# Sparse attention: two query tiles move from in front of the heads to beside them, and maxima, exponentials and value products change places in a step

## The chip, the cores and the metric

The kernel runs on one core of one Trainium2 chip. The metric is the time of one execution on the device in microseconds (us); lower is better. The kernel before took 1767.51 us in the median of three executions (1764.67 to 1768.47).

## What is computed

The reference is a decoder trunk of two layers over 256 positions of width 1024. Layer 0 is a latent attention with 16 heads and a feed-forward of product-key experts. From its output one set of keys and values is computed, for three branches. Layer 1 is the sparse attention with which the change has to do, and another expert feed-forward. Every sub-layer ends in a layer norm.

The sparse attention has 16 heads in 4 groups; the heads of a group share keys and values. Each head attends in three ways, and the results are added with sigmoid gates:

```
sc = q @ k_cmp;  p_c = masked_softmax(sc);  o_c = p_c @ v_cmp     # 15 compressed blocks
sc = q_rot @ k_g;  p_s = masked_softmax(sc);  o_s = p_s @ v_g     # selected blocks of 64 keys
sc = q_rot @ k_w;  p_w = masked_softmax(sc);  o_w = p_w @ v_w     # window of 512
out = gate0 * o_c + gate1 * o_s + gate2 * o_w
```

With 256 positions there are 4 blocks and up to 16 may be selected, so the selected branch sees every earlier key, as the window does. The kernel therefore handles both as plain causal attention with keys of their own (`br` 0 and 1). `q_rot` is the query after rotary embedding, `q` the one before. The compressed keys and values come out of a small two-layer network with a GELU over blocks of 32 tokens.

## The kernel before, in words

All large products are done as three TensorE products of a high and a low part: ScalarE rounds a float32 tile to its high part (`hi`, L119), VectorE subtracts it for the low part (`lo`, L130). Weights come through SP's DMA queue as a stream in a fixed order into four raw slots; `nxt()` takes the next tile, splits tiles ahead of it in `prep()`, and the low part of a tile frees a raw slot and so releases the next load. Each engine works strictly in the order in which the program was written; that order is written by hand.

The order around the change in `nsa` is kept by two counters. `tick()` counts one up for each weight tile or step, and `defer(n, f)` puts a piece of work n ticks later. Rotary embedding (`rope_T`) multiplies on VectorE, adds on GpSimd, and then goes through DRAM to change its layout: the store to `bounce` is issued one tick later, the load (`kr` for keys, `qr` for queries) two ticks later, both on SP. `k_split` (L1331) and `q_split` (L1342) then make high and low parts of the rotated keys and queries: casts on ScalarE, subtractions on VectorE.

There are eight query tiles, two for each group of four heads. `q_tile(i)` multiplies the residual stream with one; behind the second tile of a group come the copy `qu` and the rope. Tiles 0 to 3 stand between the four parts of `compress`, which fills the hidden layer of the compressed branch; then come tile 4, `mk_hid`, tile 5, `mk_kc` and `mk_hr` (the rest of the small network), and then a loop of 19 steps `st`. In step `st` TensorE computes the scores of head `st` (L1490 to L1498, `s0` and `s1`), transposes the scaled probabilities of head `st - 2` (two sets of three, L1500 to L1505), and in even steps from 4 on multiplies the probabilities of two heads with their values (`pvp`, L1507 on). VectorE takes the maxima of head `st` (L1523, L1524), ScalarE the exponentials (L1528, L1531), and VectorE or GpSimd scales head `st - 1` (L1541). `beside` names what else stands in a step: query tiles 6 and 7 in steps 0 and 2, and from step 6 on the output projection, one piece (`out_step`) in each even step. `cmp_at` names the four parts of the compressed branch (`cmp_scores`, `cmp_exp`, `cmp_sum`, `cmp_T`), once for each half of the heads, from steps 0 and 4 on. `out_close` ends the projection and makes the layer norm.

`self.ps()` takes one of four PSUM banks; a step's `s0`, its two sets of transposes, `pvp`, the query tiles and the compressed branch all take theirs there. `s1` has two banks of its own.

Of the kernel before, what the change touches and what calls it, by code (L numbers as in the profile page):

```python
# [12 lines left out]
F32 = mybir.dt.float32  # L13
# [5 lines left out]
AF = mybir.ActivationFunctionType  # L19
OP = mybir.AluOpType  # L20
AX = mybir.AxisListType
# [3 lines left out]
P = 128  # L25
# [18 lines left out]
class Kern:  # L44
# [1187 lines left out]
    def nsa(self, hN, gb):  # L1232
# [4 lines left out]
        with es:  # L1237
# [81 lines left out]
            for br in range(2):  # L1319
# [17 lines left out]
                self.defer(5, k_split)  # L1337
# [13 lines left out]
            def q_tile(i, tick=True):  # L1351
# [6 lines left out]
                def after():  # L1358
                    if hf == 1:
# [4 lines left out]
                        self.defer(4, lambda: q_split(g))  # L1364
# [93 lines left out]
            q_tile(4)()  # L1458
            mk_hid()
            q_tile(5)()  # L1460
            mk_kc()
            mk_hr()
# [4 lines left out]
            self.out_open(oT, hN, gb, False, 2, (x4, "x4"))  # L1467
            beside = {0: lambda: q_tile(6, False), 2: lambda: q_tile(7, False)}
            for k in range(KC - 2):
                beside[2 * k + 6] = lambda k=k: self.out_step(k)  # L1470
            cmp_at = {}
            for hb, s0_ in ((0, 0), (1, 4)):
                for i, f in enumerate((cmp_scores, cmp_exp, cmp_sum, cmp_T)):
                    cmp_at[s0_ + i] = lambda f=f, hb=hb: f(hb)
            pr, pts = {}, {}
            for st in range(NH + 3):
# [16 lines left out]
                cmp_at.get(st, lambda: None)()  # L1493
                if st == 1:
                    mk_vc()
                h = st - 2
                if 0 <= h < NH:
                    p, m = pr.pop(h)  # L1498
                    pT = prob.tile([P, 2, 384], F32, tag="pT", name="pT")
                    for br in range(2):  # L1500
                        ps = self.ps()
                        for i in range(3):
                            self.tr(ps[:, i * P:(i + 1) * P], p[:, br, i * P:(i + 1) * P])
                        nc.scalar.copy(pT[:, br, :], ps[:, 0:384])
                    pts[h] = pT  # L1505
                h = st - 3
                if 0 <= h < NH and h % 2 == 1:  # L1507
# [12 lines left out]
                h = st  # L1520
                if h < NH:
                    m = self.small.tile([P, 4, 4], F32, tag="m", name="m", bufs=4)
                    nc.vector.tensor_reduce(m[:, 0, 0:2], s0v, axis=AX.X, op=OP.max)  # L1523
                    nc.vector.tensor_reduce(m[:, 0, 2:4], s1v, axis=AX.X, op=OP.max)  # L1524
# [125 lines left out]
```

## Time and profile before

| | |
|---|---|
| median of three executions | 1767.51 us |
| profiled execution | 1764.78 us, span from the first to the last instruction 1763.0 us |
| mean granted clock of TensorE, share of full speed | 0.990 |
| TensorE busy | 1719.8 us (98%) |
| VectorE busy | 1554.6 us (88%) |
| ScalarE busy | 1043.3 us (59%) |
| GpSimd busy | 486.9 us (28%) |
| heads of the sparse attention, first scores to the last value products | 922.45 to 1005.05 us |

Times in the profile count from the first instruction. "PE" is TensorE, "PEld" its weight loads, "DVE" VectorE, "ACT" ScalarE, "POOL" GpSimd, "SPq" SP's DMA queue. L196 is the helper that issues every product, L225 the one for transposes, so tiles tell them apart: `ks,qs` are scores, `hT,hi` and `hT,lo` a query tile, `ident,p` transposes of probabilities, `pcT,vcp` and `pT,vN` value products. A busy TensorE may run at half clock, so its granted clock is read beside it. Matmuls overlap each other, so a row's start is compared with the next row's start.

### The profile page before, as it was taken

To read this page: it belongs to the slowest core of one execution; us is meant where nothing else is said; L and a number is where in the kernel's file an instruction comes from. 1 tells how busy PE (TensorE), PEld (TensorE's weight loads), DVE (VectorE), ACT (ScalarE), POOL (GpSimd) and SP (SyncE) were. 2 spreads that over 40 slices of the span, in tenths; PEclk is the share of its full clock that TensorE was granted. 3 is DMA by queue.
4 is the path that set the end of the run, shared out by engine and by line. 5 is a ranking of instruction groups with operands and counts; after the bars stand their busy time and mean duration, and the time that the engine had idled before them with its cause. 6 is when DMAs were issued, how large, how long until landed. Compare 5 with 4: busy or idle time off the path is not lost.

```text
span 1763.0 us, 30707 instructions
## 1 busy us (share of the span) xinstructions
PE 1719.8 (98%) x10610; PEld 1493.1 (85%) x10610; DVE 1554.6 (88%) x3675; ACT 1043.3 (59%) x2267; POOL 486.9 (28%) x441
## 2 busy tenths in 40 slices
PE   7999999999999999999898999999999999999997
PEld 6879999888888888888786789998888888888886
DVE  6778988988998999999677789988889997999998
ACT  6646555766666555556365755556666665655554
POOL 2110002000001777661341210001000005777840
PEclk9999999999999999999998999999999999999999
DMA  7535667555556899998571265657555557999992
GB/s 249 171 132 183 201 189 258 185 177 180 177 181 239 338 400 371 362 354 318 186 250 61 94 206 179 200 189 270 170 182 185 179 181 288 380 379 363 376 366 107
DMA packets 118619, 416.66 MB, mean 236 GB/s; under 512 B 16032, under 2 KB 18112, under 8 KB 117376
## 3 DMA queue, kind: packets, MB, share of 16 engines
q1 hardware_dynamic: 88976, 322.60, 53.6%
q0 software_dynamic: 29488, 92.10, 13.9%
q8 instruction: 84, 1.38, 0.3%
q14 instruction: 71, 0.58, 0.1%
HBM read 400.49 MB, written 13.63 MB: 235 GB/s over the span
## 4 chain that ended last, share of the span: by engine, by line
PE 88%; DVE 5%; DMA 3%; ACT 2%; issue 1%; POOL 0%; SPq 0%; ACTq 0%
PE mm L196 48%; PE acc L196 39%; PE mm L225 1%; DVE lo L130 1%; DMA raw<-p_wq 1%; ACT hi L119 1%; DMA actD<-gst 1%; DVE bnst L271 0%; DMA xT<-xT 0%; DMA raw<-s_wT 0%; POOL row L468 0%; DVE hN L293 0%; DVE hN L275 0%; DVE hN L268 0%; DMA spare<-p_v 0%
## 5 line engine op out<-in xcount | busy, mean ns | idle before, releaser
L196 PE MATMUL mm<-hT,hi 128*128 128x256 f32 (+1 forms) x3360 | 838.1, 330 | 0.0
L196 PE MATMUL mm<-hT,lo 128*128 128x256 f32 x2376 | 638.1, 280 | 1.3 <-DVE lo L130 1.3
L119 ACT CAST hi<-raw 128x1024 fp32r<-128x1024 f32 (+1 forms) x464 | 485.4, 1049 | 249.5 <-PE acc L196 102.6
L196 PEld LDWEIGHTS mm<-hT,hi 128*128 128x128 f32 x3360 | 553.4, 189 | 49.4 <-issue 1.2
L130 DVE TENSOR_TENSOR lo<-raw,hi 128x1024 fp32r<-128x1024 f32 (+1 forms) x460 | 562.1, 1225 | 35.5 <-ACT hi L119 30.8
L196 PEld LDWEIGHTS mm<-hT,lo 128*128 128x128 f32 x2376 | 448.3, 189 | 15.5 <-DVE lo L130 1.9
L196 PE MATMUL acc<-hi,W 128*128 128x512 f32 x1476 | 414.6, 389 | 0.3 <-ACT W L761 0.3
L196 PEld LDWEIGHTS acc<-hi,W 128*128 128x128 f32 x1476 | 276.9, 188 | 58.2 <-ACT W L761 0.7
L196 PE MATMUL acc<-lo,W 128*128 128x512 f32 x984 | 303.3, 389 | 0.3 <-issue 0.3
L750 POOL DMA_DIRECT2D actD<-gst x64 | 34.8, 544 | 793.5 <-ACT gst L748 793.4
L468 POOL DMA_INDIRECT row<-p_v,gidx x128 | 189.7, 1482 | 111.6 <-DVE gacc L482 63.8
L196 PEld LDWEIGHTS acc<-lo,W 128*128 128x128 f32 x984 | 184.5, 188 | 39.6 <-issue 0.9
L119 ACT CAST hi<-spare 128x1024 fp32r<-128x1024 f32 x125 | 131.3, 1051 | 115.2 <-PE acc L196 90.5
L472 POOL DMA_INDIRECT gel<-actD,gidx x128 | 172.7, 1349 | 50.2 <-issue 37.8
L482 DVE SCALAR_TENSOR_TENSOR gacc<-row,gw,gacc 128x1024 f32<-128x1024 f32 x126 | 161.5, 1282 | 1.1
L130 DVE TENSOR_TENSOR lo<-spare,hi 128x1024 fp32r<-128x1024 f32 x125 | 152.7, 1222 | 7.6 <-ACT hi L119 5.0
L742 ACT ACTIVATE mm<-mm 128x192 f32<-128x192 f32 (+23 forms) x170 | 40.9, 241 | 122.5 <-DVE mm L740 122.5
L766 DVE TENSOR_TENSOR W<-A,W 128x128 fp32r<-128x128 f32 (+1 forms) x512 | 108.1, 254 | 1.8 <-ACT W L761 1.8
L740 DVE TENSOR_TENSOR mm<-mm,half 128x256 f32<-128x256 f32 x174 | 74.7, 429 | 16.3 <-ACT half L739 15.8
L761 ACT CAST W<-A 128x192 fp32r<-128x192 f32 x256 | 88.2, 346 | 0.0
L643 DVE SCALAR_TENSOR_TENSOR A<-acc,A 128x176 f32<-128x176 f32 (+16 forms) x268 | 56.0, 274 | 34.2 <-PE acc L196 31.2
L745 ACT ACTIVATE A<-mm 128x192 f32<-128x192 f32 (+23 forms) x244 | 67.5, 277 | 7.7 <-DVE mm L740 2.6
(275 smaller groups left out, 1771.5 us busy)
## 6 DMA issues: line engine op xcount, KB each, us to landing
raw<-p_u SPq DMA_DIRECT2D x256, 512.0 KB
spare<-p_v SPq DMA_DIRECT2D x64, 1024.0 KB
raw<-p_v SPq DMA_DIRECT2D x63, 1024.0 KB
raw<-p_wq SPq DMA_DIRECT2D x32, 512.0 KB
actD<-gst POOLq DMA_DIRECT2D x64, 128.0 KB
raw<-b_wo SPq DMA_DIRECT2D x12, 512.0 KB
raw<-a_wo SPq DMA_DIRECT2D x8, 512.0 KB
raw<-s_wT SPq DMA_DIRECT2D x8, 512.0 KB
```

What stands on the lines that cost most here:

```text
L119: self.nc.scalar.copy(self.his[i], self.raws[i])
L130: e.tensor_tensor(self.los[i], raw, self.his[i].bitcast(F32), op=OP.subtract)
L196: self.nc.tensor.matmul(out, a, b, start=start, stop=stop)
L468: nc.gpsimd.indirect_dma_start(out=t, out_offset=None, in_=gtable, in_offset=bass.IndirectOffsetOnAxis(ap=gidx[:, 0, c:c + 1], axis=0))
L472: nc.gpsimd.indirect_dma_start(out=gel[c // 4][:, c % 4:c % 4 + 1], out_offset=None, in_=gplaces, in_offset=bass.IndirectOffsetOnAxis(ap=g ...
L482: nc.vector.scalar_tensor_tensor(gacc, t, gw[:, c:c + 1], gacc, op0=OP.mult, op1=OP.add)
L643: nc.vector.scalar_tensor_tensor(y, pv[:, j0:j0 + m], 1.0 / GS, y, op0=OP.mult, op1=OP.mult)
L740: nc.vector.tensor_tensor(ps[:, 0:S], ps[:, 0:S], t, op=OP.add)
L742: nc.scalar.activation(ps[:, 0:n], ps[:, 0:n], AF.Gelu)
L745: nc.scalar.activation(y[:, n:ND], ps[:, n:ND], AF.Gelu)
L761: nc.scalar.copy(WW[j][:, 0:ND], slot(j))
L766: nc.vector.tensor_tensor(WW[j][:, o:o + c.stop - c.start], slot(j)[:, c], WW[j][:, c].bitcast(F32), op=OP.subtract)
```

## The change

- `k_split` runs 4 ticks (branch 0) and 3 ticks (branch 1) behind its rope, where it was 5; `q_split` 2 ticks for group 0 and 3 for the others, where it was 4.
- Tiles 4 and 5, `mk_hid`, `mk_kc` and `mk_hr` leave the place in front of the loop. The four tiles 4 to 7 stand in steps 0, 1, 3 and 5; `mk_hid` in step 0, `mk_kc` and `mk_hr` in step 1, `mk_vc` in step 2. The compressed branch's parts begin in steps 2 and 6, where they began in 0 and 4.
- Maxima and exponentials are a function, `reduce_exp`. In steps 0 to 5 it stands in front of the compressed branch's parts; from step 6 on behind the transposes.
- The value products stand in front of the transposes of their step, where they stood behind them; the first pair comes in step 5 and not 4. The first piece of the output projection comes in step 7 and not 6.

```diff
--- before.py
+++ after.py
@@ -1334,7 +1334,7 @@
                     nc.scalar.copy(ks[64:128, :, br, :], ks[0:64, :, br, :].bitcast(F32))
                     nc.scalar.copy(klo[64:128, :, br, :], klo[0:64, :, br, :].bitcast(F32))
 
-                self.defer(5, k_split)
+                self.defer(4 - br, k_split)
 
 
             raws, qs = {}, {}
@@ -1361,7 +1361,7 @@
                         raws[g] = tmp.tile([64, HG, S], F32, tag="raw4", name="qr")
                         nc.scalar.copy(qu[:, g].rearrange("p a t -> p (a t)"), ps)
                         self.rope_T(tmp, ps.rearrange("p (a t) -> p a t", a=2), rT, raws[g])
-                        self.defer(4, lambda: q_split(g))
+                        self.defer(2 if g == 0 else 3, lambda: q_split(g))
                 return after
 
             def compress(hp, q):
@@ -1455,24 +1455,36 @@
                     self.tr(tp[:, tt * P:(tt + 1) * P], pc[:, tt, H8(hb), :].rearrange("p h c -> p (h c)"))
                 nc.scalar.copy(pcT[:, hb, :], tp[:, 0:S])
 
-            q_tile(4)()
-            mk_hid()
-            q_tile(5)()
-            mk_kc()
-            mk_hr()
             self.warm(AF.Exp)
 
 
             oT = [big.tile([P, KC, S], F32R, tag="big", name="oT") for _ in range(2)]
-            self.out_open(oT, hN, gb, False, 2, (x4, "x4"))
-            beside = {0: lambda: q_tile(6, False), 2: lambda: q_tile(7, False)}
+            self.out_open(oT, hN, gb, False, 4, (x4, "x4"))
+            beside = {st: lambda i=i: q_tile(4 + i, False) for i, st in enumerate((0, 1, 3, 5))}
             for k in range(KC - 2):
-                beside[2 * k + 6] = lambda k=k: self.out_step(k)
-            cmp_at = {}
-            for hb, s0_ in ((0, 0), (1, 4)):
+                beside[2 * k + 6 + (k == 0)] = lambda k=k: self.out_step(k)
+
+            cmp_at = {0: [mk_hid], 1: [mk_kc, mk_hr], 2: [mk_vc]}
+            for b8_, s0_ in ((0, 2), (1, 6)):
                 for i, f in enumerate((cmp_scores, cmp_exp, cmp_sum, cmp_T)):
-                    cmp_at[s0_ + i] = lambda f=f, hb=hb: f(hb)
+                    cmp_at.setdefault(s0_ + i, []).append(lambda f=f, b8_=b8_: f(b8_))
+            pv_at = {2 * k + 4 + (k == 0): 2 * k + 1 for k in range(NH // 2)}
             pr, pts = {}, {}
+
+            def reduce_exp(h, s0v, s1v):
+                m = self.small.tile([P, 4, 4], F32, tag="m", name="m", bufs=4)
+                nc.vector.tensor_reduce(m[:, 0, 0:2], s0v, axis=AX.X, op=OP.max)
+                nc.vector.tensor_reduce(m[:, 0, 2:4], s1v, axis=AX.X, op=OP.max)
+                nc.vector.tensor_scalar(m[:, 1, :], m[:, 0, :], -scale, None, op0=OP.mult)
+                p = prob.tile([P, 2, 384], F32, tag="p", name="p")
+                for br in range(2):
+                    nc.scalar.activation(p[:, br, 0:P], s0v[:, br, :], AF.Exp, bias=m[:, 1, br:br + 1], scale=scale,
+                                         accum_out=m[:, 2, br:br + 1])
+                for br in range(2):
+                    nc.scalar.activation(p[:, br, P:384], s1v[:, br, :], AF.Exp, bias=m[:, 1, 2 + br:3 + br], scale=scale,
+                                         accum_out=m[:, 2, 2 + br:3 + br])
+                pr[h] = (p, m)
+
             for st in range(NH + 3):
                 self.tick()
                 h = st
@@ -1490,21 +1502,12 @@
                     self.mm(s0v, self.identb, self.cmask, False, True)
                     self.mm(s1v[:, :, P:S], self.identb, self.cmask, False, True)
                 after = beside.get(st, lambda: None)() or (lambda: None)
-                cmp_at.get(st, lambda: None)()
-                if st == 1:
-                    mk_vc()
-                h = st - 2
-                if 0 <= h < NH:
-                    p, m = pr.pop(h)
-                    pT = prob.tile([P, 2, 384], F32, tag="pT", name="pT")
-                    for br in range(2):
-                        ps = self.ps()
-                        for i in range(3):
-                            self.tr(ps[:, i * P:(i + 1) * P], p[:, br, i * P:(i + 1) * P])
-                        nc.scalar.copy(pT[:, br, :], ps[:, 0:384])
-                    pts[h] = pT
-                h = st - 3
-                if 0 <= h < NH and h % 2 == 1:
+                if st < 6:
+                    reduce_exp(st, s0v, s1v)
+                for f in cmp_at.get(st, ()):
+                    f()
+                h = pv_at.get(st)
+                if h is not None:
                     pvp = self.ps()
                     pp = [pts.pop(h - 1), pts.pop(h)]
                     hb, g = h // 8, h // HG
@@ -1517,20 +1520,18 @@
                             self.mm(o[e], vN[:, 0, c:c + 64], pp[e][:, br, 0:S], False, False)
                         for e in range(2):
                             self.mm(o[e][:, P:S], vN[:, 1, c:c + 64], pp[e][:, br, S:384], False, br == 1)
-                h = st
-                if h < NH:
-                    m = self.small.tile([P, 4, 4], F32, tag="m", name="m", bufs=4)
-                    nc.vector.tensor_reduce(m[:, 0, 0:2], s0v, axis=AX.X, op=OP.max)
-                    nc.vector.tensor_reduce(m[:, 0, 2:4], s1v, axis=AX.X, op=OP.max)
-                    nc.vector.tensor_scalar(m[:, 1, :], m[:, 0, :], -scale, None, op0=OP.mult)
-                    p = prob.tile([P, 2, 384], F32, tag="p", name="p")
+                h = st - 2
+                if 0 <= h < NH:
+                    p, m = pr.pop(h)
+                    pT = prob.tile([P, 2, 384], F32, tag="pT", name="pT")
                     for br in range(2):
-                        nc.scalar.activation(p[:, br, 0:P], s0v[:, br, :], AF.Exp, bias=m[:, 1, br:br + 1], scale=scale,
-                                             accum_out=m[:, 2, br:br + 1])
-                    for br in range(2):
-                        nc.scalar.activation(p[:, br, P:384], s1v[:, br, :], AF.Exp, bias=m[:, 1, 2 + br:3 + br], scale=scale,
-                                             accum_out=m[:, 2, 2 + br:3 + br])
-                    pr[h] = (p, m)
+                        ps = self.ps()
+                        for i in range(3):
+                            self.tr(ps[:, i * P:(i + 1) * P], p[:, br, i * P:(i + 1) * P])
+                        nc.scalar.copy(pT[:, br, :], ps[:, 0:384])
+                    pts[h] = pT
+                if 6 <= st < NH:
+                    reduce_exp(st, s0v, s1v)
                 h = st - 1
                 if 0 <= h < NH:
                     p, m = pr[h]
@@ -1541,8 +1542,8 @@
                             eng.tensor_scalar(p[:, br, c], p[:, br, c], m[:, 3, 2 * tt + br:2 * tt + br + 1],
                                               gates[:, tt, 16 * br + 16 + h:16 * br + 17 + h], op0=OP.mult, op1=OP.mult)
                 after()
-                h = st - 3
-                if 0 <= h < NH and h % 2 == 1:
+                h = pv_at.get(st)
+                if h is not None:
                     self.split(oT[0][:, h // 2, :], oT[1][:, h // 2, :], pvp[:, 0:S])
             self.out_close()
 
```

## Rows read from the trace of the kernel before

**Rows 1.** The profile's chain that ended last, share of the span by engine.
```profile
PE 88%; DVE 5%; DMA 3%; ACT 2%; issue 1%; POOL 0%; SPq 0%; ACTq 0%
```

**Rows 2.** Windows: stretch, its length, busy us by engine (instructions), clock, DMA share, GB/s.
```profile
core 0: us, PE busy (x) PEld busy (x) DVE busy (x) ACT busy (x) POOL busy (x), PEclk, DMA share, GB/s
914.00:976.00 62.00, 52.59 (x333) 42.07 (x330) 47.94 (x113) 39.67 (x117) 9.48 (x12) 0.83 0.26 80
976.00:996.00 20.00, 19.17 (x139) 13.82 (x139) 14.89 (x40) 17.85 (x64) 10.42 (x12) 1.00 0.25 79
```

**Rows 3.** Timeline of TensorE, first heads: start, duration, instruction, [idle before <- releaser].
```profile
914.15 0.50 PE L196 MATMUL mm<-hT,hi 128*128 128x256 f32 x2
...
919.96 0.99 PE L196 MATMUL mm<-hidT,w2k 128*128 128x60 f32 x8
922.45 0.36 PE L196 MATMUL mm<-ks,qs 128*128 128x256 f32 x1 [1.49 <-DVE qs L1347]
...
927.86 1.90 PE L196 MATMUL mm<-kcp,qu 128*128 128x64 f32 x16
```

**Rows 4.** Timeline of SP's DMA queue: rope stores and loads of two groups.
```profile
908.06 0.38 SPq L1191 DMA_DIRECT2D bounce<-ropeO  x1
...
912.41 0.45 SPq L1192 DMA_DIRECT2D qr<-bounce  x1
...
925.86 0.39 SPq L1191 DMA_DIRECT2D bounce<-ropeO  x1
...
928.26 0.45 SPq L1192 DMA_DIRECT2D qr<-bounce  x1
```

**Rows 5.** Windows around the landing of group 0's query, columns as in rows 2.
```profile
913.50:915.00 1.50, 1.50 (x15) 1.03 (x12) 1.47 (x4) 0.22 (x1) 0.52 (x1) 1.00 0.57 175
915.00:918.00 3.00, 3.00 (x29) 3.00 (x28) 2.27 (x3) 2.92 (x5) 0.92 (x2) 1.00 0.00 0
```

**Rows 6.** Timeline of VectorE in the first heads, columns as in rows 3.
```profile
924.77 1.20 DVE L1404 COPY hidR<-hidT 128x240 f32<-128x240 f32 x2
...
935.38 1.29 DVE L1414 TENSOR_TENSOR vcp<-mm,m 128x512 f32<-128x512 f32 x2
936.59 0.41 DVE L1523 TENSOR_REDUCE m<-mm 128x2 f32<-128x256 f32 x1
...
937.71 0.17 DVE L1538 RECIPROCAL m<-m 128x4 f32<-128x4 f32 x1
...
939.08 1.23 DVE L130 TENSOR_TENSOR lo<-raw,hi 128x1024 fp32r<-128x1024 f32 x1
...
960.11 1.29 DVE L1347 TENSOR_TENSOR qs<-qr,qs 64x512 fp32r<-64x512 f32 x2 [0.92 <-ACT qs L1346]
```

**Rows 7.** Timeline of TensorE, one steady cycle of two heads, and the end.
```profile
974.09 0.38 PE L196 MATMUL mm<-ks,qs 128*128 128x256 f32 x1
...
975.12 0.82 PE L225 MATMUL mm<-ident,p 128*128 128x128 f32 x6
976.24 0.39 PE L196 MATMUL mm<-ks,qs 128*128 128x256 f32 x1 [0.30 <-ACT pT L1504]
...
978.68 0.82 PE L225 MATMUL mm<-ident,p 128*128 128x128 f32 x6
979.43 0.65 PE L196 MATMUL mm<-pcT,vcp 128*64 128x256 f32 x4
...
981.31 0.39 PE L196 MATMUL mm<-ks,qs 128*128 128x256 f32 x1
...
995.92 0.39 PE L196 MATMUL mm<-ks,qs 128*128 128x256 f32 x1
...
1005.05 0.73 PE L196 MATMUL acc<-hi,oT 128*128 128x512 f32 x2
```

**Rows 8.** Timeline of ScalarE in the same cycle.
```profile
972.78 0.38 ACT L1528 ACTIVATE p<-mm,m 128x128 f32<-128x128 f32 x1
...
974.37 0.40 ACT L214 CAST oT<-mm 128x256 fp32r<-128x256 f32 x1
975.70 0.86 ACT L1504 COPY pT<-mm 128x384 f32<-128x384 f32 x2 [0.93 <-PE mm L225]
```

## The prediction

> **What bounds the kernel now.** I read the chain of waits first: matmuls hold 88% of it [rows 1], so a change counts by what it does to TensorE's order, and a microsecond lost or won there is carried to the end. Then the windows of the sparse-attention stage. From 914 to 976 us TensorE is busy for 52.59 of 62 us at a mean granted clock of 0.83; the clock has two levels, 1.2 and 2.4 GHz, so a third of that stretch ran at the lower one. From 976 to 996 it is busy for 19.17 of 20 us at 1.00 [rows 2]. Two different stages stand side by side: a start of some 60 us, in which the first ten heads are slowed by short chains through VectorE and ScalarE, and a steady stretch that is full. The change acts on both, and the signs differ.
>
> **The front: heads before query tiles 4 and 5.** Before, TensorE takes up tile 4 at 914.15, is through with tiles 4 and 5, the transposes of `hb` and `mk_kc` at 920.95 (919.96 + 0.99), and waits 1.49 us for the split query of head 0 [rows 3]. After, head 0's scores come at 914.15 in its order, and 6.8 us (920.95 - 914.15) of ready work stand behind them. What is late next is the rotated query of group 0. It goes through DRAM: SP stores it at 908.06 and loads it at 912.41 [rows 4], and the data move until 915.0 [rows 5]. The `k_split` of branch 0, one tick sooner, puts three casts of ScalarE in front of the copy on which this rope waits; the key's load then ends about when they could start, and I put the delay of the copy at 0.4 us, an estimate. The second `k_split`, two ticks sooner, fills time in which ScalarE waits anyway and leaves GpSimd's rope more alone, which gives about as much back. I take a landing at 914.6. Bounds: with a store 0.8 us sooner and two trips of 2.40 us (store 925.86 to load 928.26, with little traffic [rows 4]) it lands at 912.1; with a store 0.7 us late and two trips of 4.35 at 917.5. I stay near the row of the same transfer. A cast and a subtraction of one half of the query (about 0.65 each, from the pair in [rows 6]) and 0.15 follow: scores at 916.05, between 914.15 and 918.9. TensorE waits 1.9 us where it waited 1.49. While ScalarE and VectorE stand in `q_split`, the rope of group 1 and the GELU wait behind it on both; the 6.8 us of TensorE's work cover them. Price: +0.4 us.
>
> [...]
>
> **The stretch from head 0 to head 10,** with starts in us. Head 0 916.05, 1.03 for its six products (975.12 - 974.09, [rows 7]). Tile 4 then takes 4.3 and not 2.8: before, the scores of head 0 and the tile behind them took 5.41 (927.86 - 922.45) instead of 1.03 + 2.8 (half of the 5.81 from 914.15 to 919.96, less a transpose), because the clock fell to 1.2 GHz after the idle 1.49 [rows 3]; I assume the same. Transposes 0.35, head 1 1.03, tile 5 2.8, `mk_kc` 1.0: done at 926.6. From here VectorE sets the pace, in this order: `kcp` 0.75, `mk_hr` 1.2, scaling of head 0 1.37 (939.08 - 937.71), rope 1.29, query split 1.29, maxima of head 2 1.12 (937.71 - 936.59), `vcp` 1.29, the sums of `cmp_scores` 0.75, scaling of head 1 1.37, a weight's low part 1.23, maxima of head 3 1.12, scaling of head 2 1.37 [rows 6] (the two of 0.75 and the rope are estimates, from the `vcp` and the query pair there): 14.2, so 940.8. Then ScalarE: exponentials of head 3 (1.6: 974.37 - 972.78, [rows 8]), the compressed exponential, the copies of head 1 (0.86), the cast of `q_split(2)`; VectorE's subtraction and the maxima of head 4; the exponential that frees the score bank for head 5 at 946. Tile 7 and one more fall of the clock until 951.3, `cmp_T` and its copy 0.9, the first value products 1.88 (981.31 - 979.43), transposes 0.75 (979.43 - 978.68, [rows 7]), head 6 at 955.2, compressed scores 1.7, value products 1.88, transposes 0.75, head 7 at 960.9, head 8 at 964. That is ahead of before, but at steps 7 to 9 VectorE has queued the split of `oT`, two low parts, the last `q_split`, `cmp_sum` and the maxima and scalings of heads 6 to 8 (11 us from 963, by the same rows), so head 9 comes at 969.5 and head 10 at 975.2. Before, head 10 starts at 976.24 [rows 7]. Price, the front included: -1.0 us. The query tiles moved behind the heads take along their casts, their low parts and the weight loads that these release on SP. Those loads run four slots ahead, so the output weights, first used after 960, hide that; without this cover one 4.35 us trip would show. On GpSimd's queue the rope of tile 5 now comes in front of the compressed branch's first subtraction; it is busy for 9.48 of 62 us there [rows 2].
>
> **The steady stretch: value products now in front of the transposes.** Nothing is added; only TensorE's order in even steps changes: scores, output product, value products, transposes, where the transposes came before the value products. Before, ScalarE's two copies, four exponentials and the split ran under the 1.88 us of value products and the next scores; a cycle of two heads takes 7.22 (981.31 - 974.09), with one wait of 0.30 for a copy that frees a bank [rows 7], which leaves 1.48 for the output product (7.22 less two scores, two sets of transposes, the value products and the wait). Count from the first transpose (0). The transposes end at 0.75. Four PSUM banks serve scores, transposes and value products, so the odd head's scores take the bank of the first copy, which begins at 0.58 (975.70 - 975.12) and frees it 0.54 later (976.24 - 975.70, [rows 7, 8]): 1.12, a wait of 0.37. They end at 2.15, the odd step's transposes at 2.9. The next even scores need a bank again: the first to come free is that of the next copy, which on ScalarE stands behind two copies (0.86), four exponentials (1.6) and the split (0.4) and takes 0.45, so 3.9: a wait of 1.0. Scores 1.03, output product 1.48 and value products 1.88 close the cycle at 8.3: +1.1. Head 10 at 975.2 gives its first transposes at 979.6, then head 11 at 980.7, 13 at 989.0, 15 at 997.3; before, head 15 started at 995.92. Price from head 10 to 15: +2.4.
>
> **The end.** From head 15's scores to the end of the last value products it took 9.13 (1005.05 - 995.92, [rows 7]). After, on the same count, head 14's exponentials end at 3.05, the split's low part at 3.9; VectorE then has the maxima of head 15, the scaling of 14, a low part and the scaling of 15, until 8.9; transposes, copy and value products end at 11.6, which is 10.5 after head 15's start at 1.12: +1.4. `out_close` and the second expert layer follow TensorE, and their weight loads are released by its progress, so I take no part back.
>
> Sum: -1.0 + 2.4 + 1.4 = +2.8 us, against the profiled execution's 1764.78 (span 1763.0), which lies 2.7 below the median shown, 1767.51. On that median: 1770.3. About 0.2% (3.5 us) is what a measurement can tell from no change, so this is no change, on the slow side.
>
> **Rivals.** A. *The start is worth its idle time.* For it: 9.4 us idle and a clock of 0.83 in rows 2, and the query tiles in steps 3 and 5 lie where TensorE stood still. If half the idle and half of the capacity lost to the clock (0.17 x 62 = 10.5) come back, head 10 is some 9 us early, less 3.8 for the rest: -5, 1762.5. Against it: VectorE's chain of 14 us has no holes. B. *The slow side, by the clock.* The two gaps per cycle, 0.37 and 1.0, and one of 1.3 before the last transposes are like the 1.49 after which the clock fell; that fall cost 1.5. Three cycles and the end: 2.8 + 4 x 1.5 = +8.8, 1776. Against it: the 0.30 per cycle of before left the clock at 1.00. It decides once the granted clock is below 0.95 between 976 and 1005. A landing at 917.5 in the front, with which the heads hardly begin sooner, is counted here: +5.7. C. *Value products in front cost nothing*, because a bank comes free otherwise than I read it; then only the start counts: -1, 1766.5.
>
> **Chances.** Forecast 0.45 (its own range 1766 to 1774; a third of it above 0.2%), A 0.25, B with the late landing 0.18, C 0.12. Faster: A but for 0.02, and 0.02 of C: 0.25. Slower: B and 0.15 of the forecast: 0.33. Same: 0.42. The range takes in the middle of A and of B: 1761.5 to 1776.
>
> **What would show it.** The front: head 0's scores 5 to 7 us sooner, with a wait of 1 to 3 us for VectorE's `qs`. The start: head 8 some 3 us sooner, head 10 within 2 us of before. The steady stretch: cycles of about 8.3 us with two waits of TensorE for copies, ScalarE idle before the even step's transposes. Wrong: cycles of 7.2 us (C), or head 10 more than 5 us sooner with a clock above 0.9 in the start (A).

## The result, and the profile after

The changed kernel takes 1775.23 us in the median of six executions (1772.46 to 1778.65); the kernel before, run beside it, 1766.13 (1764.12 to 1768.47). The ratio is 1.0055 [1.0043, 1.0066]: slower by 9.1 us, more than the 0.2% that a measurement can tell. The forecast of 1770.3 had the side right and the size too small: it came to +2.8.

The profiled execution after took 1774.04 us, with a span of 1772.3. Its chain that ended last, by engine, against [rows 1]:

```profile
PE 84%; DVE 7%; DMA 4%; ACT 3%; issue 1%; POOL 1%; SPq 0%; ACTq 0%; POOLq 0%
```

TensorE's share fell from 88%, so waits for VectorE and DMA entered the chain. The windows show where (columns as in [rows 2]):

```profile
914.00:976.00 62.00, 46.79 (x324) 38.16 (x324) 44.35 (x106) 34.09 (x105) 10.26 (x12) 0.89 0.28 85
976.00:996.00 20.00, 16.64 (x107) 11.41 (x106) 12.26 (x34) 14.88 (x56) 6.72 (x8) 0.91 0.20 63
996.00:1012.00 16.00, 14.26 (x108) 9.94 (x108) 10.70 (x30) 10.30 (x37) 3.36 (x4) 1.00 0.21 67
```

In the start TensorE is idle for 15.21 of 62 us where it was idle for 9.41, at a granted clock of 0.89 where it was 0.83 (a second trace of before, below, has 0.89 too); in the steady stretch it is idle for 3.36 of 20 us where it was 0.83 [rows 2]. Both stages lost. TensorE's waits in the start, with one row that has none in between, answer to [rows 3]:

```profile
918.83 0.55 PE L196 MATMUL mm<-ks,qs 128*128 128x256 f32 x1 [5.18 <-DVE qs L1347]
...
936.94 0.90 PE L225 MATMUL mm<-ident,p 128*128 128x128 f32 x3 [3.33 <-ACT p L1481]
...
948.80 0.39 PE L196 MATMUL mm<-ks,qs 128*128 128x256 f32 x1 [3.42 <-ACT p L1481]
...
955.05 0.65 PE L196 MATMUL mm<-pcT,vcp 128*64 128x256 f32 x4 [0.46 <-ACT pcT L1456]
...
978.83 0.56 PE L196 MATMUL mm<-ks,qs 128*128 128x256 f32 x1
```

These are head 0 (3.6 us sooner than before), the second of the two sets of transposes for head 0, head 5, the first compressed value products, and head 10. Three waits hold 11.9 us. Head 10 comes 2.6 us later than in [rows 7]. The first wait is the query's trip; SP's queue and then ScalarE, against [rows 4]:

```profile
908.90 0.38 SPq L1191 DMA_DIRECT2D bounce<-ropeO  x1
912.38 0.33 SPq L107 DMA_DIRECT2D raw<-b_wo  x1
912.80 0.45 SPq L1192 DMA_DIRECT2D qr<-bounce  x1
```

```profile
917.34 1.14 ACT L1346 CAST qs<-qr 64x512 fp32r<-64x512 f32 x2 [4.01 <-DMA qr<-bounce]
```

The load starts 0.4 us later than before, directly behind a weight load, and ScalarE's cast, which waits for it, begins at 917.34; that start is taken as the landing. The other two waits are for exponentials, and these wait for VectorE. Its queue in front of head 2's maxima, then ScalarE:

```profile
929.26 0.72 DVE L1399 TENSOR_TENSOR kcp<-mm,m 128x240 f32<-128x240 f32 x2 [1.80 <-PE mm L196]
...
932.97 1.81 DVE L1347 TENSOR_TENSOR qs<-qr,qs 64x512 fp32r<-64x512 f32 x2
934.82 0.42 DVE L1476 TENSOR_REDUCE m<-mm 128x2 f32<-128x256 f32 x1
```

```profile
936.08 0.37 ACT L1481 ACTIVATE p<-mm,m 128x128 f32<-128x128 f32 x1 [5.37 <-DVE m L1478]
```

Head 2's scores were through at 930.2; its maxima begin at 934.82, because `kcp`, `hidR`, a scaling, a rope and a query split stand in front of them. One steady cycle of TensorE and the end, against [rows 7]:

```profile
987.88 0.39 PE L196 MATMUL mm<-ks,qs 128*128 128x256 f32 x1 [0.79 <-ACT pT L1531]
...
993.46 0.39 PE L196 MATMUL mm<-ks,qs 128*128 128x256 f32 x1 [0.29 <-ACT pT L1531]
...
996.10 0.39 PE L196 MATMUL mm<-ks,qs 128*128 128x256 f32 x1 [0.78 <-ACT pT L1531]
...
1001.70 0.39 PE L196 MATMUL mm<-ks,qs 128*128 128x256 f32 x1 [0.30 <-ACT pT L1531]
...
1012.07 0.73 PE L196 MATMUL acc<-hi,oT 128*128 128x512 f32 x2
```

A cycle takes 8.22 us (996.10 - 987.88) where it took 7.22, with two waits for copies of transposed probabilities (0.29 and 0.78) where there was one of 0.30. The last value products end, as far as the start of the next product shows it, 10.37 us after the start of head 15's scores (1012.07 - 1001.70); before, 9.13.

So the 9.3 us between the two profiled spans are: +2.6 to head 10, +3.2 from there to head 15, +1.2 at the end, and 2.3 behind the attention. The last term is looked at first.

### The profile page after: what moved, and what is told of

It is laid out like the page before. It is cut to its first block, busy times and chain, and to the rows that moved or that the text cites. A ratio compares the mean times of both kernels' runs of the same rounds, so it can differ in the third digit from the quotient of the medians.

```text
span 1772.3 us, 30712 instructions
## 1 busy us (share of the span) xinstructions
PE 1717.1 (97%) x10610; PEld 1491.5 (84%) x10610; DVE 1552.4 (88%) x3675; ACT 1043.5 (59%) x2267; POOL 473.4 (27%) x441
## 4 chain that ended last, share of the span: by engine, by line
PE 84%; DVE 7%; DMA 4%; ACT 3%; issue 1%; POOL 1%; SPq 0%; ACTq 0%; POOLq 0%
PE mm L196 45%; PE acc L196 38%; DVE lo L130 2%; PE mm L225 1%; DMA raw<-p_wq 1%; DMA raw<-s_wT 1%; DMA actD<-gst 1%; ACT hi L119 1%; DMA xT<-xT 0%; DVE bnst L271 0%; ACT p L1484 0%; POOL row L468 0%; DVE hN L293 0%; ACT p L1481 0%; DVE hN L275 0%
## 5 line engine op out<-in xcount | busy, mean ns | idle before, releaser
L468 POOL DMA_INDIRECT row<-p_v,gidx x128 | 194.8, 1522 | 121.1 <-DVE gacc L482 84.9
L472 POOL DMA_INDIRECT gel<-actD,gidx x128 | 157.1, 1227 | 50.0 <-issue 36.9
```

The costliest lines, as they stand in the source:

```text
L468: nc.gpsimd.indirect_dma_start(out=t, out_offset=None, in_=gtable, in_offset=bass.IndirectOffsetOnAxis(ap=gidx[:, 0, c:c + 1], axis=0))
L472: nc.gpsimd.indirect_dma_start(out=gel[c // 4][:, c % 4:c % 4 + 1], out_offset=None, in_=gplaces, in_offset=bass.IndirectOffsetOnAxis(ap=g ...
```

## The experiments

Times are medians; ratios are against the kernel before in the same set of runs, whose median was 1764.23, 1763.43 and 1763.71 us in the three sets of the experiments and 1766.13 in that of the result. Starts are those of TensorE's first score product of a head. "End" is the start of the last product with `keep`, the close of the attention's projection; "rest" is the span less that.

| kernel | median | ratio | head 0 | head 5 | head 10 | head 15 | end | rest |
|---|---|---|---|---|---|---|---|---|
| before | 1766.13 | 1 | 922.5 | 955.5 | 976.2 | 995.9 | 1018.1 | 744.9 |
| before_again | 1765.17 (one) | | 921.9 | 952.6 | 974.2 | 993.9 | 1016.0 | 747.4 |
| after | 1775.23 | 1.0055 [1.0043, 1.0066] | 918.8 | 948.8 | 978.8 | 1001.7 | 1025.1 | 747.2 |
| after_again | 1774.84 (one) | | 918.1 | 948.3 | 978.3 | 1002.3 | 1025.7 | 747.4 |
| values_behind | 1770.99 | 1.0040 [1.0026, 1.0053] | 919.7 | 949.9 | 978.6 | 999.8 | 1021.9 | 746.9 |
| before_values_front | 1772.00 | 1.0044 [1.0027, 1.0061] | 922.6 | 954.1 | 977.3 | 999.3 | 1022.8 | 746.7 |
| load_first | 1774.45 | 1.0056 [1.0041, 1.0071] | 917.2 | 948.1 | 979.1 | 1001.9 | 1025.4 | 747.5 |
| qsplit2_late | 1770.86 | 1.0046 [1.0033, 1.0059] | 919.4 | 947.0 | 978.9 | 999.7 | 1021.9 | 747.2 |
| qsplit2_late_tile4 | 1776.04 | 1.0067 [1.0054, 1.0080] | 919.6 | 950.4 | 983.3 | 1004.9 | 1027.0 | 747.2 |
| before_splits | 1767.08 | 1.0017 [1.0003, 1.0031] | 929.9 | 957.0 | 976.3 | 996.5 | 1018.6 | 746.8 |
| splits_late | 1770.89 | 1.0039 [1.0025, 1.0053] | 920.7 | 948.3 | 978.5 | 999.6 | 1021.7 | 746.4 |
| exp_behind | 1778.48 | 1.0075 [1.0060, 1.0090] | 919.6 | 951.2 | 984.8 | 1006.5 | 1028.7 | 748.0 |
| late_and_behind | 1774.85 | 1.0058 [1.0045, 1.0071] | 921.4 | 950.4 | 982.5 | 1003.5 | 1025.7 | 747.9 |
| before_exp_front | 1769.83 | 1.0031 [1.0017, 1.0045] | 922.6 | 957.6 | 979.5 | 999.2 | 1021.3 | 746.7 |

My first theory: the value products in front of the transposes cost the cycles and the end, and the late landing of head 0's query costs the start. The rivals: one of the two is nothing, or the loss lies elsewhere in the start.

**after_again and before_again: how far one profiled execution goes.** No edit.

> The changed kernel once more, for a second trace. In the first trace 7.0 us of the 9.3 are lost up to the end of the sparse attention and 2.3 in the expert layer behind it, where for some 90 us three products of a group took 0.352 us instead of 0.340 at the same granted clock. If that belongs to the change, the same stretch is slow again; if it is how the chip ran then, the stretch lies elsewhere or is not there, and the time is 1772 to 1779 us.

> The kernel before, profiled once more. About 2.3 us of the 9.3 between the two profiled spans lie behind the attention, in the second expert layer: three products there took 0.340 us in the trace of before and 0.352 in that of after, at the same granted clock 1.00. If that pace belongs to the kernel before, this run shows 0.340 again and 378 us from the first to the last of the layer's gather stores, and the span is 1763. If it belongs to the single execution that was profiled, this run shows 0.352 and some 381 us, and the span is 1765 to 1766; then only the 7 us up to the end of the attention are the change's own.

The changed kernel repeats to within 0.8 us. The kernel before doesn't repeat in its parts: the second execution is 2.1 us sooner at the end of the attention and 2.5 us longer behind it. Most of the first difference arises behind head 0, which starts 0.6 us sooner in the second. Heads 0 and 1 of before_again, and its window of the start (columns as in [rows 2]):

```profile
921.89 0.36 PE L196 MATMUL mm<-ks,qs 128*128 128x256 f32 x1 [1.49 <-DVE qs L1347]
...
927.35 0.36 PE L196 MATMUL mm<-ks,qs 128*128 128x256 f32 x1
```

```profile
914.00:976.00 62.00, 51.26 (x339) 40.34 (x339) 49.22 (x117) 41.66 (x126) 10.65 (x14) 0.89 0.26 81
```

The wait of 1.49 us is the same in both executions. Behind it the granted clock was 0.54 in the first (923.4 to 927.0), so largely the lower level, and 1.00 in the second (922.8 to 926.0), and head 1 came 7.11 us behind head 0 in the one and 5.46 in the other. So the rise from 0.83 to 0.89 in the start is no gain of the change. Against before_again the start has the same clock and 15.21 us idle in place of 10.74.

Three windows of 10 us from the second expert layer, of the first trace of before and of before_again:

```profile
1100.00:1110.00 10.00, 10.00 (x90) 10.00 (x90) 10.00 (x45) 4.68 (x13) 0.55 (x1) 1.00 0.64 199
1120.00:1130.00 10.00, 10.00 (x91) 10.00 (x90) 9.97 (x49) 5.25 (x11) 0.54 (x1) 1.00 0.68 212
1140.00:1150.00 10.00, 10.00 (x90) 10.00 (x90) 9.72 (x17) 6.83 (x14) 0.54 (x1) 1.00 0.64 201
```

```profile
1100.00:1110.00 10.00, 10.00 (x88) 10.00 (x87) 10.00 (x44) 4.35 (x10) 0.55 (x1) 1.00 0.68 208
1120.00:1130.00 10.00, 10.00 (x88) 10.00 (x86) 9.97 (x54) 4.57 (x10) 0.54 (x1) 1.00 0.62 195
1140.00:1150.00 10.00, 10.00 (x87) 10.00 (x86) 9.72 (x17) 7.13 (x13) 0.54 (x1) 1.00 0.59 187
```

At the same granted clock the first did 90 or 91 products in 10 us, the second 87 or 88. The rest is 746.4 to 748.0 in all thirteen other traces, four of them of the kernel before or an edit of it; only the trace that the prediction was worked from has 744.9. So nothing behind the attention is put down to the change. Against before_again the whole 9.1 us is in the attention (1025.1 - 1016.0): +4.6 to head 10, +3.2 to head 15 (22.9 against 19.6), +1.3 behind it. That agrees with the medians, so I take 4.6 for the start and not 2.6, by this one trace.

**values_behind: the value products behind the transposes again, from step 6 on.**

```diff
+ def values(): ...   # the block at pv_at.get(st), unchanged
+ if st < 6: pvp = values()
  ...                 # transposes of head st - 2
+ if st >= 6: pvp = values()
```

> The changed kernel (1775.2 us) with one part undone: from step 6 on the value products stand behind the transposes again; step 5, the later query tiles and the maxima in front stay. Theory 1 (the order of TensorE in the even steps costs about 1 us per cycle of two heads and 1.2 us at the end): cycles of two heads go back from 8.22 us to about 7.2, head 10 to head 15 from 22.9 to about 20 us, and the kernel gains 4 to 5 us, to about 1770.7. Theory 2 (the loss is made in front, by the late query of group 0 and a late start that never closes; the order of TensorE is neutral): cycles may change, but what is saved in them is waited for elsewhere; the time stays within 1.5 us of 1775.2. Both expect head 0's scores at about 918.8 us.

```profile
987.35 0.39 PE L196 MATMUL mm<-ks,qs 128*128 128x256 f32 x1 [0.29 <-ACT pT L1537]
...
992.41 0.39 PE L196 MATMUL mm<-ks,qs 128*128 128x256 f32 x1
...
994.55 0.39 PE L196 MATMUL mm<-ks,qs 128*128 128x256 f32 x1 [0.30 <-ACT pT L1537]
...
999.75 0.39 PE L196 MATMUL mm<-ks,qs 128*128 128x256 f32 x1
```

The cycle is back at 7.20 us with one wait; the end is 3.2 us sooner, and by the ratios 2.6 us are won (0.0015 x 1765, though the two intervals overlap). Head 10 is where it was (978.6). By this the longer cycles and the longer end are one mechanism, and the start is another. Not all comes back: from head 10 to head 15 it takes 21.1 us, where I expected about 20 and before_again has 19.6, because the first cycle still takes 8.7 (978.63 to 987.35).

**before_values_front: the same edit the other way, in the kernel before.**

```diff
- h = st - 2 ...   # transposes
- h = st - 3 ...   # value products
+ h = st - 3 ...
+ h = st - 2 ...
```

> The kernel before (1766.1 us) with one part of the change alone: the value products of a step stand in front of its transposes, in all steps; all else as before. Theory 1: cycles of 8.2 us instead of 7.22, a longer end, +4.5 to +6 us, about 1771.5. Theory 2: within 1.5 us of 1766.1.

```profile
985.51 0.39 PE L196 MATMUL mm<-ks,qs 128*128 128x256 f32 x1 [0.78 <-ACT pT L1518]
...
991.10 0.39 PE L196 MATMUL mm<-ks,qs 128*128 128x256 f32 x1 [0.30 <-ACT pT L1518]
...
993.75 0.39 PE L196 MATMUL mm<-ks,qs 128*128 128x256 f32 x1 [0.78 <-ACT pT L1518]
```

The same two waits and a cycle of 8.24 us appear. Head 10 comes at 977.3, later too; in this run the value products stand in front from step 4 on. The order of these products alone makes the kernel before slower by 0.44%.

**load_first: head 0's query load in front of the weight load.**

```diff
+ if i == 3: self.tick()
- hi, lo = self.nxt(tick=tick)
+ hi, lo = self.nxt(tick=tick and i != 3)
```

> The changed kernel (1775.2 us) with one order changed: at query tile 3 the tick (the load of group 0's rotated query and its split) comes in front of the preparation of the next weight tiles, so on SP's queue the query's load no longer stands behind a weight load that waits for VectorE's low part. Theory 2 in its narrow form (the query lands late because a weight load was put right in front of it): the load takes about 2.6 us again and not 4.5, head 0's scores come at 916 to 917 us instead of 918.8, and the kernel gains 2 to 2.8 us, about 1772.7. If the late landing is hidden by later waits (theory 1 alone makes the loss): under 1 us.

```profile
915.75 1.14 ACT L1346 CAST qs<-qr 64x512 fp32r<-64x512 f32 x2 [3.72 <-DMA qr<-bounce]
917.23 0.55 PE L196 MATMUL mm<-ks,qs 128*128 128x256 f32 x1 [3.92 <-DVE qs L1347]
...
948.11 0.58 PE L196 MATMUL mm<-ks,qs 128*128 128x256 f32 x1 [3.42 <-ACT p L1483]
```

The load, issued at 912.31, takes 3.44 us. Head 0 is 1.6 us sooner, head 5 0.7, head 10 not at all. The wait in front of head 5 is the same 3.42 us. The second half of my theory falls: the late landing is real, but a microsecond won there isn't carried to head 10.

That left the start open. The next theory: VectorE's queue in front of the maxima sets the pace of heads 2 to 5. Its rival: the products that the change moves behind head 5 cost the start, and a wait that is taken away in front of head 5 comes back later.

**qsplit2_late: values_behind, with group 2's query split two ticks later.**

```diff
- self.defer(2 if g == 0 else 3, lambda: q_split(g))
+ self.defer(2 if g == 0 else 5 if g == 2 else 3, lambda: q_split(g))
```

> After with the value products behind the transposes (the earlier run values_behind, 1770.99 us) and the query split of group 2 two ticks later, where VectorE stands idle for 4.7 us. Theory (VectorE's queue sets the pace of heads 2 to 5): head 4's maxima no longer stand behind that split (2.7 us with its wait), so TensorE's wait of 3.42 us before head 5 falls below 1 us, the clock stays up in tile 7 (some 1.5 us more), and head 10 starts at 974 to 976 where values_behind had 978.6: 1766.5 to 1768.5 us. Rival (the start is bound by the compressed branch in steps 6 to 9, and the lead won at head 5 is given back there): head 5 comes sooner, head 10 still at 978 or later, 1770 to 1772 us.

```profile
946.95 0.39 PE L196 MATMUL mm<-ks,qs 128*128 128x256 f32 x1 [0.81 <-ACT p L1481]
953.17 0.65 PE L196 MATMUL mm<-pcT,vcp 128*64 128x256 f32 x4 [2.05 <-ACT pcT L1456]
...
970.16 1.00 PE L225 MATMUL mm<-ident,p 128*128 128x128 f32 x6 [0.81 <-DVE p L1550]
```

The wait in front of head 5 fell from 3.42 to 0.81 as the theory said, and head 5 came 3.0 us sooner. The next wait, for the compressed branch's transposed probabilities (`pcT`), rose from 0.46 to 2.05, another of 0.81 appeared, and head 10 stayed at 978.9: from head 5 to head 10 TensorE waits 6.3 us in all, where it waited 3.6 in values_behind. The rival's numbers, not the theory's. ScalarE's rows show what `pcT` waits for:

```profile
951.14 0.37 ACT L1481 ACTIVATE p<-mm,m 128x128 f32<-128x128 f32 x1 [1.62 <-DVE m L1547]
...
952.73 0.38 ACT L1456 COPY pcT<-mm 128x256 f32<-128x256 f32 x1
```

TensorE's transposes for `pcT` were through at 951.1 (950.74 + 0.38). Their copy stands on ScalarE behind head 5's exponentials, which wait for VectorE, because in steps 0 to 5 of the new order the exponentials come in front of the compressed branch's parts.

**qsplit2_late_tile4: the same, with query tile 4 in front of the loop.**

```diff
+ q_tile(4)()
- self.out_open(oT, hN, gb, False, 4, (x4, "x4"))
+ self.out_open(oT, hN, gb, False, 3, (x4, "x4"))
- beside = {st: lambda i=i: q_tile(4 + i, False) for i, st in enumerate((0, 1, 3, 5))}
+ beside = {st: lambda i=i: q_tile(5 + i, False) for i, st in enumerate((0, 3, 5))}
```

> The same as qsplit2_late, and query tile 4 back in front of the loop, where TensorE waits 5.2 us for head 0's query. Theory (the front's wait is lost capacity, and VectorE's chain of 14 us begins when mk_kc is through): 2.8 us of products go into the wait, the chain begins up to 1.8 us sooner, head 10 comes 1.5 to 3 us sooner than in qsplit2_late: 1764 to 1767 us. Rival (the query's landing sets everything, TensorE has slack): head 0 at the same time, head 5 and head 10 within 0.7 us of qsplit2_late, and the same time within 1 us.

```profile
919.60 0.55 PE L196 MATMUL mm<-ks,qs 128*128 128x256 f32 x1 [3.27 <-DVE qs L1347]
...
935.81 1.94 PE L196 MATMUL mm<-w2v,hidR 128*128 128x64 f32 x8 [6.68 <-ACT p L1482]
```

Both expectations miss: head 10 comes 4.4 us later than in qsplit2_late. The wait for head 0 shrank from 5.57 to 3.27, but one of 6.68 appears in step 2. VectorE stood still for 2.37 us up to 932.34 for the split of group 1: tile 4's place changes the count of ticks, so that split now waited in VectorE's queue for its cast (and the cast 3.11 us for the query's load), with head 1's maxima and `kcp` behind it. The run changed more than the one thing that it was to test, and on that it says little.

**before_splits: the kernel before with the sooner key and query splits alone.**

```diff
- self.defer(5, k_split)
+ self.defer(4 - br, k_split)
- self.defer(4, lambda: q_split(g))
+ self.defer(2 if g == 0 else 3, lambda: q_split(g))
```

> The kernel before with only the key and query splits at the change's sooner places (4 and 3 ticks for the keys, 2 and 3 for the queries). Theory (in before, ScalarE's late key split makes head 0 wait 1.49 us, and the clock falls after it): head 0 starts at 921 with less than 0.5 us of wait, the clock stays up behind it, heads 1 to 10 come 1.5 to 3 us sooner: 1763 to 1765 us. Rival (the sooner splits make ScalarE and VectorE wait for the key's and the query's trips, and the GELU and the hidden layer's copies stand behind them): TensorE waits for mk_hid instead, head 0 is no sooner than 922, 1766 to 1769 us.

```profile
923.42 0.69 PE L225 MATMUL mm<-ident,hb 128*128 128x128 f32 x2 [7.40 <-ACT hb L1384]
...
929.86 0.37 PE L196 MATMUL mm<-ks,qs 128*128 128x256 f32 x1
```

The rival's wait, larger than it said: ScalarE stands in the query's split, the GELU behind it, and TensorE waits 7.40 us. Head 0 is 8.0 us later than in before_again, yet head 10 only 2.1 and the end 2.6: the start swallows most of a delay in front of it. The time is 1.0017 [1.0003, 1.0031].

**splits_late, exp_behind and late_and_behind: which part of the change costs the start.** All three start from values_behind. The first moves the splits back (in group 0 as far as its order allows), the second puts maxima and exponentials behind the transposes in steps 0, 1, 3 and 4 (in steps 2 and 5 the four PSUM banks don't allow it), the third does both.

```diff
- self.defer(4 - br, k_split)
+ self.defer(5, k_split)
- self.defer(2 if g == 0 else 3, lambda: q_split(g))
+ self.defer(3 if g == 0 else 4, lambda: q_split(g))
```

```diff
- if st < 6: reduce_exp(st, s0v, s1v)
+ if st in (2, 5): reduce_exp(st, s0v, s1v)
  ...
- if 6 <= st < NH: reduce_exp(st, s0v, s1v)
+ if st < NH and st not in (2, 5): reduce_exp(st, s0v, s1v)
```

> values_behind (after with the value products behind the transposes, 1770.99 us, head 10 at 978.6) with the key and query splits back at later places: 5 ticks for the keys, 3 for the query of group 0 (the latest that its order allows), 4 for the others. Theory (a split stands on ScalarE and VectorE in front of what the next head needs): the split of group 1 no longer stands in front of head 2's maxima, TensorE's wait of 3.33 us in step 2 falls to about 1.5, the GELU no longer waits behind a split, head 10 comes at 975 to 977, 1767 to 1769.5 us. Rival (what TensorE does between heads 0 and 5 was cut down by moving products behind head 5, and from there it is full, so waits in front of head 5 only change places): head 10 at 978 to 979.5, 1770 to 1772 us.

> values_behind with maxima and exponentials behind the transposes again in steps 0, 1, 3 and 4 (in 2 and 5 the banks of PSUM ask for the front). Theory (their place in front costs the start, because copies and the compressed branch's parts stand behind exponentials that wait for VectorE): the waits of 3.33 and 3.42 us fall to about 1 each, head 10 at 975 to 977, 1767 to 1769.5 us. Rival (the place is nearly indifferent, the order of the tiles and of the compressed branch decides): head 10 within 1 us of 978.6, 1770 to 1772.5 us.

> splits_late and exp_behind together: of the change there stand only the tiles, the small network and the compressed branch at their later steps, the first value products in step 5 and the splits one tick sooner for groups 0 to 3. If what costs the start are the splits or the place of the exponentials, this is within 2 us of the kernel before (head 10 at 974 to 976, 1764 to 1767 us). If it is the work moved behind the first heads, head 10 stays at 978 or later, 1770 to 1772 us, and by that cause is settled as the order of the tiles.

Waits of TensorE in the start, of splits_late, of exp_behind and of late_and_behind:

```profile
937.58 0.55 PE L225 MATMUL mm<-ident,p 128*128 128x128 f32 x3 [1.79 <-ACT p L1481]
...
948.27 0.39 PE L196 MATMUL mm<-ks,qs 128*128 128x256 f32 x1 [0.80 <-ACT p L1481]
...
956.21 1.12 PE L196 MATMUL mm<-pcT,vcp 128*64 128x256 f32 x4 [3.78 <-ACT pcT L1456]
```

```profile
940.56 0.90 PE L225 MATMUL mm<-ident,p 128*128 128x128 f32 x3 [2.98 <-ACT p L1481]
...
959.65 1.12 PE L196 MATMUL mm<-pcT,vcp 128*64 128x256 f32 x4 [4.26 <-ACT pcT L1456]
```

```profile
941.05 0.90 PE L225 MATMUL mm<-ident,p 128*128 128x128 f32 x3 [1.44 <-ACT p L1481]
...
959.65 1.12 PE L196 MATMUL mm<-pcT,vcp 128*64 128x256 f32 x4 [5.12 <-ACT pcT L1456]
```

splits_late: the waits for exponentials fell to 1.79 and 0.80, and the wait for `pcT` rose to 3.78; the time is that of values_behind. So the place of the splits is worth nothing there. exp_behind, with head 10 at 984.8 outside both expectations, is 0.35% slower than values_behind (1.0075 against 1.0040, intervals apart), and late_and_behind about 0.2% slower than splits_late (1.0058 against 1.0039; the intervals overlap, but its end is 4.0 us later): in the new order the front place of the exponentials wins some 3 to 6 us, where I had expected it to be indifferent or to cost. late_and_behind holds, of the change, the new steps of tiles, small network, compressed branch and first value products, with group 0's query split one tick sooner and the exponentials of heads 2 and 5 in front. It is 10 us slower than before (0.0058 x 1764), slower than I expected in either case, and head 10 comes 8.3 us later than in before_again. So the cost of the start comes with the new order of this work, and the rest of the change gives part of it back. How much of it is the moved products alone isn't separated: the wait of 5.12 us is again for the copy of `pcT`, which stands behind head 5's exponentials in this run too.

**before_exp_front: the kernel before with maxima and exponentials in front in steps 0 to 5.**

```diff
+ if st < 6: reduce_exp()
  cmp_at.get(st, lambda: None)()
  ...
+ if 6 <= st < NH: reduce_exp()
```

> The kernel before with maxima and exponentials in front of the compressed branch's parts in steps 0 to 5, and nothing else. If this place costs nothing by itself: head 10 at 974 to 976, 1762 to 1766 us. If it does (the compressed branch's sums and maxima come later on VectorE, and its transposes then wait): head 10 at 977 or later, 1767 to 1769 us. If it helps (head 2 and 3 sooner): head 10 at 973 or sooner, 1760 to 1762 us.

```profile
939.96 0.38 PE L196 MATMUL mm<-ks,qs 128*128 128x256 f32 x1 [2.34 <-ACT p L1501]
...
947.37 0.58 PE L196 MATMUL mm<-ks,qs 128*128 128x256 f32 x1 [2.98 <-ACT p L1501]
```

In the old order the same place costs 0.31%: waits of 2.34 and 2.98 us for exponentials appear in front of heads 3 and 4, of the kind of the 3.33 and 3.42 after, and head 10 is 5.2 us later than in before_again. No kernel here beat the one before.

## Why the prediction was right in its side and wrong in its size

- **The front, +0.4.** The mechanism held: a wait for the split query, whose trip is late next. The term was mis-sized: landing 917.34 and not 914.6, wait 5.18 and not 1.9, inside the bounds that were given. The prediction put the copy's delay at 0.4, with as much given back, which makes 915.0 and not the 914.6 that it took; the copy came 1.84 us later (904.51 against 902.67), the store 0.84 and the load 0.39. The 915.0 itself is where the data stop moving; in the later traces the cast that waits for the load begins about 1 us behind that (load_first: no data move after 914.7, cast at 915.75; after: 916.3 and 917.34). The load was queued behind a weight load at 912.38, and then took 4.54 us (912.80 to 917.34). In load_first, in front of that weight load, it took 3.44 (912.31 to 915.75). No run makes this term count at head 10: load_first won 1.6 of it and lost them again.
- **From head 0 to head 10, -1.0 with the front.** This is the step that failed: +2.6 by the rows, +4.6 by before_again. Its chain had the right lengths: 30.0 us from head 0 to head 5 forecast and measured (948.80 - 918.83), 29.2 to head 10 against 30.0, VectorE's 14.2 us of work against 14.1 (929.26 to 943.34). In its own sum the 3.6 us by which head 10 was missed (978.8 against 975.2) are 2.8 of head 0's late start and 0.8 of the way from there; another 2.0 is the place of before's head 10, which it took from a trace that has it at 976.2, where before_again has 974.2. But in load_first a head 0 that is 1.6 us sooner brings no sooner head 10, so no run shows that the size of the front counts there. What was wrong is the conclusion that heads which begin sooner end sooner. Before head 5 the change leaves out some 7 us of products that the kernel before did there: query tile 7 (2.8), the second half's compressed scores (1.9), the first value products (1.9), two compressed transposes (0.4). Head 5 came only 3.8 us sooner (948.8 against 952.6), as TensorE's waits from head 0's up to it rose from 7.8 in before_again (6.5 in the first trace) to 12.3. Behind head 5 the 7 us are then due on a TensorE that is busy, at a granted clock of 1.00 and with one wait of 0.30 from 960 to 972: head 5 to head 10 took 30.0 us, against 21.6. Up to head 10 the products are the same in both orders; TensorE's waits in front of them add up to 16.8 us after and 10.6 in before_again. A busy TensorE is not the whole cause: in qsplit2_late, with head 5 sooner still, the lead was lost in waits.
- **The steady stretch, +2.4.** Right in mechanism: the cycle was forecast at 8.3 and measured 8.22, with waits of 0.37 and 1.0 forecast and 0.30 and 0.79 measured. The term came to 3.2, 0.8 more, because the first cycle of it, head 10 to head 12, took 9.05: the granted clock was 0.56 to 0.59 from 977 to 981, behind waits of 1.32 us for the second half's compressed probabilities and 1.07 for a scaled head. Before has the same two waits (1.20 and 1.07) and such a fall of the clock (0.50 from 969 to 971) in front of head 10, and values_behind keeps its own at 979 to 981; so this 0.8 goes with the start and not with the order of the value products.
- **The end, +1.4.** Measured 1.24.
- **The rest, 0.** Right for the change, wrong for the trace: the profiled execution of before had a start 2.1 us longer, 1.65 of it behind head 0's wait, where its clock fell, and an expert layer 2.5 us shorter than before_again. Its span gave the right total, so no sum over the whole showed it, and my start was set against the longer one.
- **Rival A** (the start gives its idle time back) fell: 15.21 us idle in place of 9.41. **Rival C** fell: 8.22 per cycle. **Rival B** came near in time (1776) but not in cause. Its test, a clock below 0.95 between 976 and 1005, was met (0.91 up to 996), yet values_behind and qsplit2_late, without the two gaps per cycle, show that same dip at 978, and from 996 to 1012, gaps and all, the clock is 1.00. Nor did the gap from which it took its price always bring a fall: before_again has the wait of 1.49 without one. The measured 1775.23 lies in the stated range only by this rival's end of 1776, and outside the forecast's own 1766 to 1774; that is luck. Its variant of a landing at 917.5 happened, at 917.34, and was not the price.

What stays open: which chain in the new order binds head 10. The first compressed `pcT` is there at 955.05 after and was at 946.04 before; the waits that were taken away came back in front of its first use in qsplit2_late and splits_late. The rows of qsplit2_late put that wait down to the place of `pcT`'s copy behind head 5's exponentials, not to the compressed branch being late. Putting that copy in front of those exponentials, and moving the compressed branch, the tiles or the first value products alone back to their old steps in the new order, were not tried.

## What to carry to other kernels

Put the operations whose results pass through another engine first and the long independent products behind them: here 1.9 us of value products behind the transposes hide two copies, and in front of them cost 1 us per cycle in either kernel. To begin a chain sooner is worth only what it saves at its end; add up the work that a full engine still has to do behind the point where the lead is read. Where a forecast is a few microseconds, two profiled executions of the kernel before are worth more than another decimal: their parts differed here by 2 us in opposite senses under equal spans.

## What the runs showed of the hardware that was not expected

The same products of the same program ran at 91 or at 87 per 10 us in the same stretch, both at a granted clock of 1.00; what sets that is not shown here. Behind the same wait of 1.49 us in the same program the granted clock fell to the lower level in one execution (0.54 over the 3.6 us behind head 0's scores) and stayed at 1.00 in the other; that was worth 1.65 us at head 1. And the same edit, exponentials in front, made one order some 5.5 us slower (before_exp_front) and another 3 to 6 us quicker (against exp_behind and late_and_behind): the price of a place in the order depends, here, on the rest of the order.
